# Hybrid attention, LRU and convolution trunk: the positions of the block compression as a block of their own

## The chip, the core and the metric

One core of one Trainium2 chip runs the whole program. The metric is device microseconds of one execution, the median over several runs. Engines are named as the profile names them: PE is TensorE (PEld its weight loads), DVE is VectorE, ACT is ScalarE, POOL is GpSimd, SP is SyncE, whose queue issues almost all DMAs.

## The reference, cut to what matters

Two layers, 512 tokens, model width 1024. Each layer normalises, projects to 4376 columns, and feeds three groups of heads (sparse attention, an RG-LRU, a Conformer convolution) that end in one output projection. The sparse attention compresses keys and values of overlapping blocks of 32 tokens, 16 apart (31 blocks, 2 groups of heads), with a position table that is the same for every block:

```python
    n_cmp = (T - L_CMP) // S_CMP + 1                      # 31
    idx = cmp_start[:, None] + jnp.arange(L_CMP)[None, :]
    def compress(kv, pos, w1, w2):
        blk = (kv[:, :, idx] + pos).reshape(B, N_KV, n_cmp, L_CMP * HEAD_DIM)
        return jax.nn.silu(blk @ w1) @ w2                 # w1: 2048 x 256, w2: 256 x 64
    kc = compress(k_c, cmp_pos[0], cmp_w1[0], cmp_w2[0])
    vc = compress(v_c, cmp_pos[1], cmp_w1[1], cmp_w2[1])
```

Since `pos` is the same for all blocks, `(kv + pos) @ w1` equals `kv @ w1` plus one row `pos @ w1` that is added to every block.

## The kernel before, in words

Everything is float32. A product that has to be exact to float32 is made of three matmuls on rounded parts: a matrix is split into a high part (a rounding copy on ACT, helper `cast`, L156) and a low part (the difference, on DVE, helper `lower`, L159). For weights, `w_split` makes both in tiles of 128 x 1024 called whi and wlo, three buffers each; one raw load of 1 MB (two buffers) yields two such pairs. A unit of projection (`proj`, L208 to 216) is 24 matmuls of 512 columns, eight times whi, whi, wlo, into one accumulator.

PE's order and that of all engines is, outside the attention, set by a scheduler of the build: it lists the instructions of each engine once, in advance, and each engine then works its list strictly in order. The code of a layer is written in the order of L981 to L1004: the gated units, q, the inputs of the compression (`do_kv`), keys, `do_prep(0)`, the LRU's inputs and gates (`do_u_lru`), `do_prep(1)`, `do_main(0)` with the four units of z_nsa between its parts, the LRU scan, `do_main(1)` with the units of z_lru, then the 30 taps for each of four channel tiles of the depthwise convolution (`conv_taps`, L422 on DVE, 120 a layer), which the scheduler spreads into whatever places DVE's list has.

The compression, for keys (c = 0) and values (c = 1):

- `do_prep(c)` turns the 32 x 64 position table by a transpose on PE (L639) and copies it into posT (L641, 128 x 16), and fetches the tokens into ee (called ce in the trace; rows are a token's parity and channel, columns the token pairs). For each half hf of the 16 token pairs of a block it adds posT to 31 overlapping windows of ee, once for each group of heads (L650, two instructions on DVE; neighbouring outputs are read 8 floats apart), and splits the sum cM into M (tile cMs; cast on ACT, lower at L655 on DVE): 62 high columns, 62 low columns for each of 8 token pairs j.
- `do_main(c)` multiplies: for each half, each j and each of whi and wlo, one matmul with M's 124 columns as weights and 256 columns of w1 moving (L675, 16 a half), all into one accumulator ph of 124 rows. It is copied (hs, L678), and a product with the 0/1 matrix `fold` (L681) adds the high row and the low row of a block and turns the result. What follows (L684 to L703) is the hidden layer's swish and the second product.

Around this on DVE: `u_lru` filters the LRU's inputs (L545), `gate` makes its gates (L578, L583), `do_scan` its products and scans (L589, L590), `z_nsa` closes the z_nsa units (L600). On ACT: L540, L542 evacuate the LRU's inputs, L574 to L582 its gates, L612 a square root, L599 the tanh of z_nsa.

Of the kernel before, what the change touches and what calls it, by code (L numbers as in the profile page):

```python
# [8 lines left out]
F32 = mybir.dt.float32  # L9
F32R = mybir.dt.float32r  # L10
# [3 lines left out]
OP = mybir.AluOpType  # L14
# [37 lines left out]
def tile_hybrid_trunk(ctx, tc, x_in, positions, norm_g, w_in, b_gate, cmp_pos, cmp_w1, cmp_w2, lru_conv_w,  # L52
# [4 lines left out]
    V, S, G, PE, SP = nc.vector, nc.scalar, nc.gpsimd, nc.tensor, nc.sync  # L57

    const = ctx.enter_context(tc.tile_pool(name="const", bufs=1))
# [8 lines left out]
    def big(name, dt=F32, tag="t"):  # L68
        return main.tile([128, 512], dt, name=name, tag=tag, bufs=TAGS[tag])

    def pair(name, dt=F32):
        return main.tile([128, 2, 512], dt, name=name, tag="p", bufs=TAGS["p"])
# [19 lines left out]
    for t in (ident, identb):  # L92
        G.affine_select(t, zeros[:, :128], pattern=[[1, 128]], compare_op=OP.not_equal, fill=1.0, base=0,
                        channel_multiplier=-1)
    G.memset(mask[:, :384], 0.0)
    G.affine_select(maskb, zeros[:, :128], pattern=[[-1, 128]], compare_op=OP.is_ge, fill=BIG, base=0,
                    channel_multiplier=1)
    G.affine_select(cmask, zeros[:, :128].rearrange("p (i n) -> p i n", i=4), pattern=[[128, 4], [-16, 32]],
                    compare_op=OP.is_ge, fill=BIG, base=-31, channel_multiplier=1)
    G.affine_select(seen, ones, pattern=[[0, 1]], compare_op=OP.is_ge, fill=0.0, base=-31, channel_multiplier=1)  # L100

    fold = const.tile([124, 2, 32], F32, name="fold")
    G.memset(fold, 0.0)
    for g in range(2):
        for half in range(2):
            G.affine_select(fold[:, g, :31], fold[:, g, :31], pattern=[[-1, 31]], compare_op=OP.not_equal, fill=1.0,
                            base=-31 * g - 62 * half, channel_multiplier=1)
    vcz = const.tile([128, 2, 2, 64], F32R, name="vcz")
    G.memset(vcz.bitcast(F32), 0.0)

# [44 lines left out]
    def cast(out, in_):  # L155
        S.copy(out, in_)  # L156

    def lower(out, in_, hi, eng=None):
        (eng or V).tensor_tensor(out, in_, hi.bitcast(F32), op=OP.subtract)  # L159
# [208 lines left out]
    def layer(l, X, o):  # L368
# [88 lines left out]

        def out_rows(X, t, n, W, M):
            p = acc()
            mh, ml = M  # L460
            m = 0
# [8 lines left out]

        def out_proj(X, kt0, M):

# [159 lines left out]
        CMP = {}  # L632

        def do_prep(c):

            pos = work.tile([16, 128], F32, name="pos", tag="oe", bufs=1)
            SP.dma_start(out=pos, in_=cmp_pos[l, c].rearrange("(j s) d -> j (s d)", s=2))
            pt = psum.tile([128, 16], F32, name="pt", tag="tr", bufs=2)
            PE.transpose(pt, pos, ident[:16, :16])  # L639
            posT = work.tile([128, 16], F32, name="posT", tag="posT", bufs=1)  # L640
            V.tensor_copy(posT, pt)  # L641
            ee = big("ce").rearrange("p (g m) -> p g m", g=2)
            for g in range(2):
                for s in range(2):
                    SP.dma_start(out=ee[s * 64:s * 64 + 64, g],
                                 in_=KV[c][g * 64:g * 64 + 64, s * 256:s * 256 + 256])
            for hf in range(2):
                m32 = big("cM")[:, :496].rearrange("p (j g n) -> p j g n", j=8, g=2)
                for g in range(2):
                    V.tensor_tensor(m32[:, :, g, :], ee[:, g, hf * 8:hf * 8 + 248].rearrange("p (n j) -> p j n", j=8),  # L650
                                    posT[:, hf * 8:hf * 8 + 8].unsqueeze(2).to_broadcast([128, 8, 31]), op=OP.add)
                m32 = m32.rearrange("p j g n -> p j (g n)")
                M = pair("cMs", F32R).rearrange("p a b -> p (a b)")[:, :992].rearrange("p (j n) -> p j n", j=8)
                cast(M[:, :, 0:62], m32)
                V.tensor_tensor(M[:, :, 62:124], m32, M[:, :, 0:62].bitcast(F32), op=OP.subtract)  # L655
                CMP[c, hf] = M

        def do_main(c, between):

            w2 = big("w2")[:, :256].rearrange("p (a o d) -> p a o d", a=2, o=2)  # L660
            for o in range(2 - c):
                SP.dma_start(out=w2[:, :, o, :], in_=cmp_w2[l, c].rearrange("(a p) d -> p a d", p=128))
            ph = psum.tile([128, 256], F32, name="pt", tag="tr", bufs=2)
            for hf in range(2):
                for _ in range(2):
                    next(between)
                r = raw_tile().rearrange("p (k c) -> p k c", c=256)
                SP.dma_start(out=r, in_=cmp_w1[l, c, hf * 1024:(hf + 1) * 1024, :].rearrange("(j p) c -> p j c", p=128))
                M = CMP[c, hf]
                for a in range(2):  # L670
                    hi, lo = w_split(r[:, 4 * a:4 * a + 4, :])
                    for k in range(4):
                        j = 4 * a + k
                        for w in (hi, lo):
                            PE.matmul(ph[:124], M[:, j], w[:, k], start=hf == 0 and j == 0 and w is hi,  # L675
                                      stop=hf == 1 and j == 7 and w is lo)
            hs = big("hs")[:124, :256]
            S.copy(hs, ph[:124])  # L678
            ph = psum.tile([128, 2, 64], F32, name="pt", tag="tr", bufs=2)
            for a in range(2):  # L680
                PE.matmul(ph[:, a], hs[:, a * 128:a * 128 + 128], fold.rearrange("p g n -> p (g n)"), start=True,  # L681
                          stop=True)
            hid = work.tile([128, 2, 64], F32, name="hid", tag="m")
            S.activation(hid, ph, AF.Tanh, scale=0.5)  # L684
            V.scalar_tensor_tensor(hid, hid, 1.0, ph, op0=OP.add, op1=OP.mult)
            if c == 0:
                pk = psum.tile([128, 2, 32], F32, name="pt", tag="tr", bufs=2)
                for a in range(2):
                    PE.matmul(pk.rearrange("p g n -> p (g n)"), w2[:, a].rearrange("p o d -> p (o d)"), hid[:, a, :],
                              start=a == 0, stop=a == 1)  # L690
                S.activation(KCH, pk, AF.Copy, scale=0.5)
                V.scalar_tensor_tensor(KCL, pk, 0.5, KCH.bitcast(F32), op0=OP.mult, op1=OP.subtract)
            else:
                pk = psum.tile([64, 64], F32, name="pt", tag="tr", bufs=2)
                for a in range(2):
                    PE.matmul(pk, hid[:, a, :], w2[:, a, 0, :], start=a == 0, stop=a == 1)

                for g in range(2):
                    b = slice(g * 32, g * 32 + 32)
                    S.activation(vcz[b, g, 0], pk[b], AF.Copy, scale=0.5)  # L700
                    V.scalar_tensor_tensor(vcz[b, g, 1], pk[b], 0.5, vcz[b, g, 0].bitcast(F32), op0=OP.mult,
                                           op1=OP.subtract)
                    S.copy(vcz[64 + g * 32:96 + g * 32, g], vcz[b, g].bitcast(F32))  # L703
# [284 lines left out]
        do_k()  # L988
        do_qs(1)
        do_prep(0)  # L990
        do_ks()
        do_u_lru()
# [51 lines left out]
```

## Time and profile before

| | |
|---|---|
| median of 3 runs | 774.03 us (773.87 to 775.85) |
| the profiled execution | 773.8 us, of which the span is 772.1 us |
| granted TensorE clock, mean | 0.998 of full |
| PE busy | 736.6 us, 95% of the span |
| DVE busy | 677.0 us, 88% |
| ACT busy | 460.3 us, 60% |
| POOL busy | 110.8 us, 14% |

The span starts with the first instruction and ends with the last; 1.7 us lie around it. A row of the timeline gives the start of a run of like instructions, how long they took together, the engine, line and operation, what was written from what, and in brackets the idle time of the engine just before with what ended it. Consecutive instructions of an engine overlap a little, so what one costs its queue is the distance from its start to the next start. All times of the text are of the first layer unless said; the second layer shows the same stretch 375 us later.

### The profile page before, as it was taken

What the parts mean: (1) busy time and instruction counts of PE and PEld (TensorE: products, weight loads), DVE (VectorE), ACT (ScalarE), POOL (GpSimd) and SP (SyncE); (2) the same over time, 40 slices, a digit from 0 to 9 for tenths busy, and PEclk for the clock granted to TensorE, in tenths of its full rate; (3) what the DMA queues carried; (4) which work ended last, traced back from release to release, by engine and by line L of the source; (5) the groups of instructions that cost most, each with busy time, mean ns of one, the idle gap of its engine ahead of it and who ended that gap; (6) DMA issues with size and microseconds to landing.
All of it is one profiled execution on the core that took longest, in us unless ns stands there. A gap on an engine that the chain in (4) does not pass through costs nothing.

```text
span 772.1 us, 10892 instructions
## 1 busy us (share of the span) xinstructions
PE 736.6 (95%) x3736; PEld 600.8 (78%) x3736; DVE 677.0 (88%) x1355; ACT 460.3 (60%) x891; POOL 110.8 (14%) x180
## 2 busy tenths in 40 slices
PE   7999999999999999999999999999999999999895
PEld 5788887677887787887798888776788787788774
DVE  5979999999997788988874999999999877899776
ACT  5443667684445567777652248669634375787663
POOL 2000000000001233444210000000000103344440
PEclk9999999999999999999999999999999999999999
DMA  6433285647441300103431334671855131010002
GB/s 216 137 110 106 58 212 133 178 137 248 127 154 61 113 2 2 54 2 87 168 111 56 109 104 116 191 199 34 265 182 164 54 106 59 1 56 1 2 27 110
DMA packets 68277, 82.01 MB, mean 106 GB/s; under 512 B 6633, under 2 KB 56873, under 8 KB 68222
## 3 DMA queue, kind: packets, MB, share of 16 engines
q1 hardware_dynamic: 68220, 81.31, 34.3%
q8 instruction: 30, 0.49, 0.3%
q14 instruction: 25, 0.20, 0.1%
q10 hardware_dynamic: 2, 0.00, 0.0%
HBM read 67.67 MB, written 4.19 MB: 93 GB/s over the span
## 4 chain that ended last, share of the span: by engine, by line
PE 70%; DVE 16%; ACT 8%; issue 4%; POOL 1%; DMA 1%; POOLq 0%; ACTq 0%; DVEq 0%
PE acc L214 44%; PE acc L464 9%; PE po L865 3%; PE pt L850 3%; ACT P L839 3%; PE acc L308 2%; DVE wlo L159 2%; PE ps L826 1%; PE ps L825 1%; DVE cv L422 1%; PE acc L763 1%; ACT whi L156 1%; DVE P L837 1%; PE pt L675 1%; DVE m L877 1%
## 5 line engine op out<-in xcount | busy, mean ns | idle before, releaser
L214 PE MATMUL acc<-H,whi 128*128 128x512 f32 x1024 | 325.6, 398 | 0.0
L214 PEld LDWEIGHTS acc<-H,whi 128*128 128x128 f32 x1024 | 191.4, 188 | 47.2 <-issue 1.9
L214 PE MATMUL acc<-H,wlo 128*128 128x512 f32 x512 | 203.6, 399 | 2.1 <-DVE wlo L159 2.1
L156 ACT CAST whi<-raw 128x1024 fp32r<-128x1024 f32 x102 | 106.7, 1050 | 161.4 <-PE acc L214 130.6
L422 DVE SCALAR_TENSOR_TENSOR cv<-sg,dww,cv 128x493 f32<-128x493 f32 (+18 forms) x240 | 165.4, 732 | 0.9
L159 DVE TENSOR_TENSOR wlo<-raw,whi 128x1024 fp32r<-128x1024 f32 x102 | 124.6, 1224 | 22.5 <-ACT whi L156 21.8
L214 PEld LDWEIGHTS acc<-H,wlo 128*128 128x128 f32 x512 | 96.3, 188 | 27.1 <-DVE wlo L159 3.5
L843 POOL TENSOR_SCALAR P<-P,hm,gt 128x384 f32<-128x384 f32 (+3 forms) x128 | 87.1, 687 | 131.4 <-DVE hm L841 114.7
L839 ACT ACTIVATE P<-P,hm 128x384 f32<-128x384 f32 (+2 forms) x96 | 59.0, 615 | 10.1 <-DVE hm L837 9.2
L221 POOL TENSOR_TENSOR mv<-mv,power 128x1 f32<-128x1 f32 x8 | 4.2, 546 | 419.2 <-DVE mv L725 419.2
L852 ACT CAST pt<-pt 128x512 fp32r<-128x512 f32 (+1 forms) x88 | 47.8, 546 | 23.5 <-PE pt L850 22.5
L853 DVE TENSOR_TENSOR pt<-pt 128x512 fp32r<-128x512 f32 (+1 forms) x88 | 55.7, 635 | 4.4 <-ACT pt L852 4.2
L837 DVE CUSTOM_DVE_ANT_0 P<-ps,mask 128x384 f32<-128x384 f32 (+2 forms) x96 | 51.9, 548 | 5.0 <-PE ps L826 4.4
L850 PE MATMUL pt<-ident,P 128*128 128x128 f32 x320 | 50.4, 274 | 5.0 <-DVE cs L787 3.9
L850 PEld LDWEIGHTS pt<-ident,P 128*128 128x128 f32 x320 | 38.6, 140 | 14.4 <-POOL P L843 5.7
L865 PEld LDWEIGHTS po<-pt,vv 128*128 128x128 f32 x304 | 43.8, 189 | 5.9 <-DVE pt L853 1.6
L865 PE MATMUL po<-pt,vv 128*128 128x256 f32 (+1 forms) x304 | 47.1, 289 | 0.7 <-DVE pt L853 0.7
L826 PE MATMUL ps<-KL,QS 128*128 128x384 f32 (+3 forms) x128 | 39.3, 322 | 0.0
L825 PE MATMUL ps<-KH,QS 128*128 128x384 f32 (+3 forms) x128 | 39.2, 321 | 0.0
L468 DVE TENSOR_TENSOR x<-x,acc 128x512 f32<-128x512 f32 x48 | 32.6, 680 | 0.6 <-PE acc L464 0.5
L464 PE MATMUL acc<-whi,mn 128*128 128x512 f32 x96 | 31.4, 406 | 0.3 <-DVE mn L881 0.3
L430 ACT COPY rs<-ru 32x512 f32<-32x512 f32 x48 | 29.7, 618 | 0.8
(242 smaller groups left out, 1213.1 us busy)
## 6 DMA issues: line engine op xcount, KB each, us to landing
raw<-in_w_in_dram SPq DMA_DIRECT2D x30, 1024.0 KB
raw<-in_w_out_dram SPq DMA_DIRECT2D x12, 1024.0 KB
raw<-in_cmp_w_dram SPq DMA_DIRECT2D x8, 1024.0 KB
x<-in_x_dram SPq DMA_DIRECT2D x8, 512.0 KB
raw<-in_w_in_dram SPq DMA_DIRECT2D x4, 512.0 KB
QS<-rs SPq DMA_DIRECT2D x8, 256.0 KB
QS<-ru SPq DMA_DIRECT2D x8, 256.0 KB
KH<-rs SPq DMA_DIRECT2D x8, 256.0 KB
```

What stands on the lines that cost most here:

```text
L156: S.copy(out, in_)
L159: (eng or V).tensor_tensor(out, in_, hi.bitcast(F32), op=OP.subtract)
L214: PE.matmul(p, w[k], h[k], start=n == 0, stop=n == 23)
L422: V.scalar_tensor_tensor(a[:, s:], u[:, :T - s], dww[:, ct, j:j + 1], a[:, s:], op0=OP.mult, op1=OP.add)
L464: PE.matmul(p, h[:, k], w, start=m == 0, stop=m == 11)
L837: V.tensor_tensor_reduce(p, sc[:, r, :], mask[:, 512 - L:], 1.0, BIG, OP.add, OP.min, hm[:, 0, r:r + 1])
L839: S.activation(p, p if i else sc[:, r, :], AF.Exp, scale=-1.0, bias=hm[:, 0, r:r + 1], accum_out=hm[:, 1, r:r + 1])
L843: G.tensor_scalar(P[:, r * L:(r + 1) * L], P[:, r * L:(r + 1) * L], hm[:, 2, r:r + 1], GA[i][:, h0 + r, 1 + b:2 + b], op0=OP.mult, op1=OP. ...
L850: PE.transpose(pt[:, kb, :], P[:, kb * 128:(kb + 1) * 128], ident)
L852: S.copy(dst[0], src)
L853: V.tensor_tensor(dst[1], src, dst[0].bitcast(F32), op=OP.subtract)
L865: PE.matmul(po, v, PT[w][:, kb].rearrange("p r q -> p (r q)"), start=False, stop=last and kb == i and w == 1)
```

## The change

The position table enters as a 32nd block of each group. M now has 128 columns for each j, ordered high/low, group, block: columns 0 to 30 of a group are the windows of ee, cast and lowered straight from ee for both groups in one instruction each, and column 31 is posT, cast and lowered in two small instructions of its own. The sum cM is gone. The matmuls of `do_main` then make, beside the 31 rows of blocks, a row of the positions, and `fold`, now 128 rows high, has ones that add row 31 of the first group (high and low) to all 62 blocks. Lines behind `fold` are two higher in the changed file, up to `do_prep`.

```diff
-    fold = const.tile([124, 2, 32], F32, name="fold")
+    fold = const.tile([128, 2, 32], F32, name="fold")
     G.memset(fold, 0.0)
-    for g in range(2):
-        for half in range(2):
+    for half in range(2):
+        for g in range(2):
             G.affine_select(fold[:, g, :31], fold[:, g, :31], pattern=[[-1, 31]], compare_op=OP.not_equal, fill=1.0,
-                            base=-31 * g - 62 * half, channel_multiplier=1)
+                            base=-64 * half - 32 * g, channel_multiplier=1)
+        G.affine_select(fold[:, :, :31], fold[:, :, :31], pattern=[[0, 2], [0, 31]], compare_op=OP.not_equal, fill=1.0,
+                        base=-64 * half - 31, channel_multiplier=1)
...
             for hf in range(2):
-                m32 = big("cM")[:, :496].rearrange("p (j g n) -> p j g n", j=8, g=2)
-                for g in range(2):
-                    V.tensor_tensor(m32[:, :, g, :], ee[:, g, hf * 8:hf * 8 + 248].rearrange("p (n j) -> p j n", j=8),
-                                    posT[:, hf * 8:hf * 8 + 8].unsqueeze(2).to_broadcast([128, 8, 31]), op=OP.add)
-                m32 = m32.rearrange("p j g n -> p j (g n)")
-                M = pair("cMs", F32R).rearrange("p a b -> p (a b)")[:, :992].rearrange("p (j n) -> p j n", j=8)
-                cast(M[:, :, 0:62], m32)
-                V.tensor_tensor(M[:, :, 62:124], m32, M[:, :, 0:62].bitcast(F32), op=OP.subtract)
-                CMP[c, hf] = M
+                M = pair("cMs", F32R).rearrange("p a b -> p (a b)").rearrange("p (j w g n) -> p j w g n", j=8, w=2, g=2)
+                for n, src in ((slice(0, 31), ee[:, :, hf * 8:hf * 8 + 248].rearrange("p g (n j) -> p j g n", j=8)),
+                               (slice(31, 32), posT[:, hf * 8:hf * 8 + 8].unsqueeze(2).unsqueeze(3)
+                                .to_broadcast([128, 8, 2, 1]))):
+                    cast(M[:, :, 0, :, n], src)
+                    lower(M[:, :, 1, :, n], src, M[:, :, 0, :, n])
+                CMP[c, hf] = M.rearrange("p j w g n -> p j (w g n)")
...
-                            PE.matmul(ph[:124], M[:, j], w[:, k], start=hf == 0 and j == 0 and w is hi,
+                            PE.matmul(ph, M[:, j], w[:, k], start=hf == 0 and j == 0 and w is hi,
                                       stop=hf == 1 and j == 7 and w is lo)
-            hs = big("hs")[:124, :256]
-            S.copy(hs, ph[:124])
+            hs = big("hs")[:, :256]
+            S.copy(hs, ph)
```

The scheduler also lists the instructions of this stretch in another order, on every engine. Three places show it. Names are those of the code with a number for each buffer; cv are the accumulators of the convolution, xc and rg the LRU's, zn the z_nsa results. In the changed file the lines L159, L422, L583, L589, L590 and L600 are L161, L424, L585, L591, L592 and L602.

DVE, from the first LRU scan of the layer on, before. wlo_1403 is the low part of the second half of the weights of the first compression product, wlo_1417 and wlo_1449 those of the third and the fourth z_nsa unit:

```order
L590 SCALAR_TENSOR_TENSOR xc0_1123<-xc0_1123,rg_1204 128x512
L590 SCALAR_TENSOR_TENSOR xc1_1159<-xc1_1159,rg_1204 128x512
L422 SCALAR_TENSOR_TENSOR cv2_695<-sg2_630,dww_392,cv2_695 128x501
L159 TENSOR_TENSOR wlo_1403<-raw_1388,whi_1402 128x1024
L583 SCALAR_TENSOR_TENSOR rr_1265<-sq_1288,rr_1265 128x512
L159 TENSOR_TENSOR wlo_1417<-raw_1414,whi_1416 128x1024
L650 TENSOR_TENSOR cM_1307<-ce_1302,posT_1300 128x8x31
L650 TENSOR_TENSOR cM_1313<-ce_1302,posT_1300 128x8x31
L159 TENSOR_TENSOR wlo_1449<-raw_1414,whi_1448 128x1024
```

The same place in the changed kernel, up to the third z_nsa unit (wlo_1405 and wlo_1419 are what wlo_1403 and wlo_1417 were):

```order
L592 SCALAR_TENSOR_TENSOR xc0_1127<-xc0_1127,rg_1208 128x512
L161 TENSOR_TENSOR cMs_1311<-posT_1304,cMs_1311 128x8x2
L592 SCALAR_TENSOR_TENSOR xc1_1163<-xc1_1163,rg_1208 128x512
L424 SCALAR_TENSOR_TENSOR cv2_701<-sg2_636,dww_398,cv2_701 128x503
L585 SCALAR_TENSOR_TENSOR rr_1269<-sq_1292,rr_1269 128x512
L424 SCALAR_TENSOR_TENSOR cv2_701<-sg2_636,dww_398,cv2_701 128x504
L161 TENSOR_TENSOR wlo_1405<-raw_1390,whi_1404 128x1024
L161 TENSOR_TENSOR wlo_1419<-raw_1416,whi_1418 128x1024
```

A small lowering of the positions, one more tap and the gate's product now stand ahead of the low weights, and the taps are two further on (503 where 501 was).

DVE, directly behind that, in the changed kernel; wlo_1451 is what wlo_1449 was:

```order
L424 SCALAR_TENSOR_TENSOR cv2_701<-sg2_636,dww_398,cv2_701 128x505
L591 SCALAR_TENSOR_TENSOR rg_1270<-rg_1270,rr_1269 128x512
L161 TENSOR_TENSOR cMs_1311<-ce_1306,cMs_1311 128x8x2x31
L161 TENSOR_TENSOR cMs_1316<-ce_1306,cMs_1316 128x8x2x31
L161 TENSOR_TENSOR cMs_1316<-posT_1304,cMs_1316 128x8x2
L592 SCALAR_TENSOR_TENSOR xc2_1201<-xc2_1201,rg_1270 128x512
L591 SCALAR_TENSOR_TENSOR rg_1270<-rg_1270,rr_1269 128x512
L602 SCALAR_TENSOR_TENSOR zn_1356<-zn_1356,acc_1331 128x512
L602 SCALAR_TENSOR_TENSOR zn_1356<-zn_1356,acc_1363 128x512
L161 TENSOR_TENSOR wlo_1451<-raw_1416,whi_1450 128x1024
```

Two instructions stood between the low weights of the third and of the fourth unit; now nine do.

PE at the second half of the first compression product in the changed kernel (before, all 16 matmuls of L675 stood together, and the first two matmuls of both the third and the fourth unit behind them):

```order
L675 MATMUL pt_1324<-whi_1404,cMs_1070 128x256
L216 MATMUL acc_1422<-H00_126,whi_1418 128x512
L216 MATMUL acc_1422<-H10_128,whi_1418 128x512
L675 MATMUL pt_1324<-wlo_1405,cMs_1070 128x256
```

and where the fourth unit begins, 22 matmuls of the third unit later:

```order
L216 MATMUL acc_1454<-H00_126,whi_1450 128x512
L216 MATMUL acc_1454<-H10_128,whi_1450 128x512
L675 MATMUL pt_1324<-whi_1483,cMs_1075 128x256
L216 MATMUL acc_1454<-H00_126,wlo_1451 128x512
```

Two matmuls of the third unit moved ahead of the seven that need wlo_1405; the fourth unit's third matmul in this list needs wlo_1451.

## Rows read from the trace of the kernel before

**Rows 1.** The page, part 1: busy time, share of the span, instructions.
```profile
PE 736.6 (95%) x3736; PEld 600.8 (78%) x3736; DVE 677.0 (88%) x1355; ACT 460.3 (60%) x891; POOL 110.8 (14%) x180
```
**Rows 2.** Busy time by stretches: length, PE, PEld, DVE, ACT, POOL, clock, DMA, GB/s.
```profile
155.00:165.00 10.00, 8.54 (x43) 6.97 (x42) 10.00 (x14) 9.92 (x13) 0.00 (x0) 1.00 0.05 13
165.00:175.00 10.00, 10.00 (x47) 8.13 (x46) 10.00 (x16) 8.10 (x10) 0.00 (x0) 1.00 0.91 297
```
**Rows 3.** Waits of PE, whole span: us in total, times, longest.
```profile
PE pt L675 <- DVE wlo L159: 2.9, 2, 1.5
...
PE acc L214 <- DVE wlo L159: 2.1, 2, 1.1
```
**Rows 4.** Timeline of PE: start, us, instruction, count, idle before.
```profile
164.59 0.38 PE L675 MATMUL pt<-wlo,cMs 128*124 128x256 f32 x1 [1.46 <-DVE wlo L159]
...
166.44 0.40 PE L214 MATMUL acc<-H,wlo 128*128 128x512 f32 x1
...
176.70 0.28 PE L675 MATMUL pt<-whi,cMs 128*124 128x256 f32 x1
...
178.49 0.28 PE L675 MATMUL pt<-wlo,cMs 128*124 128x256 f32 x1
...
180.79 0.50 PE L214 MATMUL acc<-H,wlo 128*128 128x512 f32 x1 [1.04 <-DVE wlo L159]
```
**Rows 5.** Timeline of DVE, from the fourth LRU channel tile on.
```profile
147.79 0.75 DVE L545 SCALAR_TENSOR_TENSOR xc<-lu,prm,xc 128x509 f32<-128x509 f32 x1
...
159.83 0.68 DVE L589 SCALAR_TENSOR_TENSOR rg<-rg,rr 128x512 f32<-128x512 f32 x1
160.43 2.33 DVE L590 TENSOR_TENSOR_SCAN xc<-xc,rg 128x512 f32<-128x512 f32 x2
162.68 0.72 DVE L422 SCALAR_TENSOR_TENSOR cv<-sg,dww,cv 128x501 f32<-128x501 f32 x1
163.31 1.22 DVE L159 TENSOR_TENSOR wlo<-raw,whi 128x1024 fp32r<-128x1024 f32 x1
164.45 0.68 DVE L583 SCALAR_TENSOR_TENSOR rr<-sq,rr 128x512 f32<-128x512 f32 x1
165.05 1.22 DVE L159 TENSOR_TENSOR wlo<-raw,whi 128x1024 fp32r<-128x1024 f32 x1
...
173.06 1.87 DVE L600 SCALAR_TENSOR_TENSOR zn<-zn,acc 128x512 f32<-128x512 f32 x3
```
**Rows 6.** Timeline of ACT.
```profile
146.97 0.79 ACT L542 ACTIVATE xc<-acc,prm 128x512 f32<-128x512 f32 x1
...
160.74 1.04 ACT L156 CAST whi<-raw 128x1024 fp32r<-128x1024 f32 x1
```
**Rows 7.** Durations by line or tile: ns min/median/max, first and last start, forms.
```profile
L650 DVE TENSOR_TENSOR cM<-ce,posT x16: 631/647/683, 123.8 to 544.1; 128x248 f32<-128x248 f32 x16
L655 DVE TENSOR_TENSOR cMs<-cM,cMs x8: 660/680/701, 128.3 to 545.8; 128x496 fp32r<-128x496 f32 x8
...
L156 ACT CAST cMs<-cM x8: 602/612/615, 127.5 to 544.8; 128x496 fp32r<-128x496 f32 x8
...
L641 DVE COPY posT<-pt x4: 164/167/172, 121.3 to 517.5; 128x16 f32<-128x16 f32 x4
...
L799 DVE TENSOR_TENSOR cp<-cp,sm x8: 415/421/426, 265.7 to 735.0; 128x256 f32<-128x256 f32 x8
```
**Rows 8.** Timeline of PE in the attention: matmuls with 128-column weights.
```profile
335.51 1.10 PE L865 MATMUL po<-pt,vv 128*128 128x256 f32 x8
```
**Rows 9.** Timeline of POOL and of SP's queue.
```profile
3.14 0.70 POOL L106 TENSOR_SCALAR_AFFINE_SELECT fold<-fold 124x31 f32<-124x31 f32 x4
5.76 0.55 POOL L221 TENSOR_TENSOR ss<-ss,power 128x1 f32<-128x1 f32 x1 [1.93 <-DVE ss L353]
...
168.55 0.37 SPq L171 DMA_DIRECT2D raw<-in_w_in_dram x1
```
**Rows 10.** The chain of work that ended last, in order of time.
```profile
181.29 0.39 PE pt L681 x4
```

## The prediction

> **What bounds the kernel.** I read the page first, then the busy time by stretches, the waits and the timelines of PE and DVE. PE is busy 95% of the span [rows 1], so time is gained or lost where PE waits, or where it has more to do. The place of the change shows such waits. Between 155 and 165 us DVE is busy 10.00 of 10 us and ACT 9.92, while PE has 8.54 [rows 2]: PE is short of operands there, and the two engines that make them are full. PE's waits name the operand: it waits for wlo, the low part of weights, at the compression product, twice in the span [rows 3]. In the first layer that is 1.46 us until 164.59, and again 1.04 us until 180.79 at a z unit [rows 4]. The second layer does the same, so the stretch costs 2.5 us a layer, 5.0 in all. DVE's list says why: the wlo that PE needs starts at 163.31, right behind two scans and a tap, with no idle time before it [rows 5], although the high part it is subtracted from was cast at 160.74 to 161.78 [rows 6]. In this stretch PE's time is the sum of DVE's list.
>
> **The parts without effect on the path.** PE's weights have 128 columns in place of 124. The 16 matmuls of a half start 0.119 us apart (176.70 to 178.49) [rows 4]; eight with 128 columns and as many moving columns take 1.10 us, 0.117 apart after the last one's 0.28 [rows 4, 8]. That adds nothing. The taller copy hs and the taller fold product move the same number of columns. POOL gets two more selects of `fold`, at 0.18 each by the four that take 0.70; POOL then idles 1.93 us before the first norm needs it [rows 9]. Without that cover the start would be 0.4 later. The number of DMAs is unchanged. The load of the next z weights, issued at 168.55 [rows 9], needs the buffer that the fourth unit's wlo releases, and on SP's queue it also falls behind one tile of x; with the times below it goes out at about 174.9, takes 3.5 us by 1 MB at 297 GB/s [rows 2], and ACT can use it only from 180.0. If it came later than that, it would replace the last wait below.
>
> **What the new instructions cost.** Of the old sum, an instruction of 248 elements took 0.65 us; one of 256 with the same kind of broadcast operand but neighbouring reads took 0.42 [rows 7]. So the broadcast costs nothing and the reads 8 floats apart cost 0.23 for 248. On its queue an instruction costs 0.08 less than its duration (1.22 from 163.31, next start 164.45) [rows 5]. The new lowering has 496 such reads: 0.60 (L655's 0.68 less 0.08) plus twice 0.23, 1.06. Its bounds are 0.60, if the reads cost nothing there, and 1.14, twice an L650. I take 1.06, since the reads are the same ones. [...] The small instructions for the positions I price by the copy of posT, 0.16 less overlap, about 0.10 [rows 7], 0.17 at most. For each half DVE loses two L650 (0.57 each) and an L655 (0.60), 1.74, and gains 1.16: 0.6 us saved, eight times. ACT's cast, 0.61 before [rows 7], may take up to 1.1 with those reads; it has 1.9 of 10 us free between 165 and 175 [rows 2], so two of them and two small ones (1.3 more) fit there.
>
> **The order decides.** All of that saving would be PE's if the lists kept their order. They don't.
> - *Up to the fourth LRU tile.* From the copy of posT (121.3 us) [rows 7] to the first filter step of that tile (147.79) [rows 5] DVE loses four L650 and two L655, 3.48, and gains two lowerings and two small ones, 2.32; but two taps of 0.63 (162.68 to 163.31) [rows 5] are drawn in ahead, 1.26, and ACT's small cast of the positions stands ahead of copies that DVE waits for, 0.17. Together +0.27: it starts at about 148.06. Earlier than 147.76 it can't, since ACT's L542 writes its operand until then [rows 6].
> - *To the second half's low weights.* Before, 15.52 us from there to 163.31 [rows 5]. Now a tap (0.63), the gate's product (0.60) and a small lowering (0.10) are ahead: start 148.06 + 15.52 + 1.33 = 164.91, end 166.13, PE goes on at 166.19 in place of 164.59. ACT casts the high part behind two gate steps of at most 0.79 [rows 6] and the small cast, from 162.5 at the latest; that is in time. Seven matmuls take PE 0.92 (1.85 to 166.44 [rows 4] less four of 0.233, the spacing of the 44 up to 176.70); the next wlo, right behind, lets it go on at 167.33.
> - *To the fourth unit's low weights.* 22 matmuls of 0.233, two more and one of 0.12: PE wants wlo_1451 at 173.05. On DVE a wlo (1.14), a tap, two LRU products (1.20), two lowerings (2.12), a small one, a scan (1.13) and two L600 (1.20) stand ahead: 166.05 + 7.52 = 173.57, end 174.79, PE at 174.85. **That is a new wait of 1.80 us**, where PE had none. Behind it 22 matmuls and 15 of the product end at 181.77, against 178.61 before (178.49 + 0.12): 3.16 late.
> - *To the z unit's low weights.* DVE: three wlo (3.42), two L600 (1.20), a scan, five taps (3.15): start 173.57 + 8.90 = 182.47, PE goes on at 183.75, after a wait of 0.9 that answers to the old 1.04. By then PE has also done the fold product, 0.39 [rows 10], which came behind this wait before. Delay 183.75 - 0.39 - 180.79 = 2.57.
>
> Behind this the list is as before, and DVE, lighter, has slack. Two layers: **5.1 us slower**. The profiled execution (773.8: span 772.1 and 1.7 around it) would be 778.9; the median of the runs is 0.2 above it, so 779.2. With the lowering at 0.60 the first step is held at 147.79 by ACT, the later ones gain another 0.92, and the delay is 1.38 a layer: 776.8. With 1.14 and small ones of 0.17 it is 3.2 a layer: 780.4.
>
> **The rivals.**
> - *Faster, 769.0.* DVE and ACT are the engines PE waits for, and DVE is relieved; if that reached PE, both old waits would go, 5.0 us. [...] The point at which it decides is the low weights of the second half: they would have to be there when PE arrives, at 163.13 (164.59 less 1.46) [rows 4], 1.4 us earlier than before. Against it: the fourth LRU tile pins DVE at 147.76, and only things that were added stand between.
> - *No change, 774 to 776.3.* The lowering costs 0.60 and DVE makes up another 0.4 a layer, because the drawn-in taps are missing later and the last wait shrinks; or the attention, where PE has short waits of its own, takes part of the delay. For it: the 0.9 at the last step is short. Against it: PE has no more idle time than 5% [rows 1].
>
> **How the numbers follow.** A measurement here tells about 0.3%, 2.3 us, from no change: faster is below 771.7, slower above 776.35. My forecast has 0.78, no change 0.13, faster 0.09. The range reaches from 775.0, inside the case of no change, to 782.0: the upper bound of 780.4 and one more wait of 0.8 a layer, since what ACT and the loads do in the new order is known by bounds only.
>
> **What would show it.** Waits of PE on wlo in the projection units rise from 1.04 us a layer to about 3, the longest near 1.8, some 10 us behind the first compression product begins; the lowering from ce reads about 1.15 us; DVE's busy time falls by some 5 us, ACT's rises by 2 to 5. The step is wrong if the first wait ends before 165.5 or the fourth unit's wlo starts before 172; then DVE isn't the sum I take it for. If the wlo come late as computed but the span doesn't grow, the delay is given back later.

## The result and the profile after

| | before | after |
|---|---|---|
| median of the runs | 774.07 us (773.87 to 775.85, 4 runs) | 781.17 us (779.78 to 781.37, 4 runs) |
| the profiled execution, and its span | 773.8, 772.1 | 779.78, 777.6 |
| granted TensorE clock, mean | 0.998 | 0.996 |

The ratio is 1.0084, 95% interval 1.0072 to 1.0097: slower, as forecast (779.2; range 775.0 to 782.0), and by more than the forecast said. Busy time on the page of the changed kernel, which answers to [rows 1]:

```profile
PE 740.3 (95%) x3736; PEld 602.1 (77%) x3736; DVE 672.3 (86%) x1347; ACT 465.3 (60%) x899; POOL 110.8 (14%) x182
```

DVE has 4.7 us less to do and ACT 5.0 more; the kernel has become slower with less work on the engine that PE waits for. PE's busy time rose by 3.7 with the same 3736 matmuls, which is explained below. PE's waits in the whole span (us, times, longest), against [rows 3]:

```profile
PE pt L675 <- DVE wlo L161: 2.2, 2, 1.1
...
PE acc L216 <- ACT whi L158: 1.7, 4, 0.6
...
PE acc L216 <- DVE wlo L161: 1.3, 2, 1.1
...
PE pt L675 <- ACT whi L158: 0.5, 2, 0.3
```

The waits on wlo add up to 3.5 us, where they were 5.0: by this view alone the kernel should be faster. What happened is on PE's timeline of the second layer (all rows of the stretch with idle time ahead of them, and three that the text uses: the third unit's first low weights, the lone matmul at 551.28, and the z unit's first low weights):

```profile
541.41 0.38 PE L675 MATMUL pt<-whi,cMs 128*128 128x256 f32 x1 [0.23 <-ACT whi L158]
542.36 0.74 PE L216 MATMUL acc<-H,whi 128*128 128x512 f32 x2 [0.56 <-ACT whi L158]
544.17 0.39 PE L675 MATMUL pt<-wlo,cMs 128*128 128x256 f32 x1 [1.07 <-DVE wlo L161]
...
545.30 0.50 PE L216 MATMUL acc<-H,wlo 128*128 128x512 f32 x1
...
551.28 0.38 PE L675 MATMUL pt<-whi,cMs 128*128 128x256 f32 x1
552.81 0.51 PE L216 MATMUL acc<-H,wlo 128*128 128x512 f32 x1 [1.14 <-DVE wlo L161]
...
561.41 0.50 PE L216 MATMUL acc<-H,whi 128*128 128x512 f32 x1 [0.29 <-ACT whi L158]
561.77 0.50 PE L216 MATMUL acc<-H,wlo 128*128 128x512 f32 x1
```

PE now stops five times a layer where it stopped twice [rows 4], at operands of both engines. The same stretch by windows, from the first matmul of the first compression product to the z unit's second pair of high weights: first the kernel before, then the changed one (length, PE busy, its matmuls; then PEld, DVE, ACT, POOL, clock, the share of the DMA engines, GB/s).

```profile
536.99:556.57 19.58, 17.03 (x89) 13.86 (x88) 19.58 (x26) 14.02 (x18) 0.00 (x0) 1.00 0.66 215
```
```profile
540.08:562.11 22.03, 18.58 (x90) 14.19 (x89) 22.03 (x28) 16.05 (x21) 0.00 (x0) 1.00 0.60 200
```

The stretch holds the same work and became 2.45 us longer: 0.90 of it is idle time of PE and 1.55 is "busy". A matmul of 256 columns inside a run starts 0.12 after the one ahead of it, and the row of one that stands alone shows 0.38 (541.41, 551.28); each stop so hides part of the delay in busy time. The delay can't be read from the idle time of PE, only from what DVE's list does. DVE is busy in all 22.03 us. Its rows at the operands (first layer, then the second):

```profile
148.92 0.75 DVE L547 SCALAR_TENSOR_TENSOR xc<-lu,prm,xc 128x509 f32<-128x509 f32 x1
...
165.67 2.36 DVE L161 TENSOR_TENSOR wlo<-raw,whi 128x1024 fp32r<-128x1024 f32 x2
167.94 0.74 DVE L424 SCALAR_TENSOR_TENSOR cv<-sg,dww,cv 128x505 f32<-128x505 f32 x1
...
169.20 2.07 DVE L161 TENSOR_TENSOR cMs<-ce,cMs 128x496 fp32r<-128x496 f32 x2
...
174.18 1.24 DVE L161 TENSOR_TENSOR wlo<-raw,whi 128x1024 fp32r<-128x1024 f32 x1
...
542.90 2.35 DVE L161 TENSOR_TENSOR wlo<-raw,whi 128x1024 fp32r<-128x1024 f32 x2
...
551.54 2.35 DVE L161 TENSOR_TENSOR wlo<-raw,whi 128x1024 fp32r<-128x1024 f32 x2
...
560.50 2.35 DVE L161 TENSOR_TENSOR wlo<-raw,whi 128x1024 fp32r<-128x1024 f32 x2
```

To price the stretch in every kernel I use two landmarks on ACT, ahead of it and behind it: the evacuation of the fourth LRU channel tile (L542 before, L544 after) and the last evacuation of the z_conv units of the layer (L628, L630). Before, then after:

```profile
231.82 0.59 ACT L628 ACTIVATE zc<-acc 128x512 f32<-128x512 f32 x1
...
522.09 0.79 ACT L542 ACTIVATE xc<-acc,prm 128x512 f32<-128x512 f32 x1
...
606.85 0.58 ACT L628 ACTIVATE zc<-acc 128x512 f32<-128x512 f32 x1
```
```profile
147.82 0.79 ACT L544 ACTIVATE xc<-acc,prm 128x512 f32<-128x512 f32 x1
...
235.13 0.59 ACT L630 ACTIVATE zc<-acc 128x512 f32<-128x512 f32 x1
...
525.14 0.79 ACT L544 ACTIVATE xc<-acc,prm 128x512 f32<-128x512 f32 x1
...
612.46 0.59 ACT L630 ACTIVATE zc<-acc 128x512 f32<-128x512 f32 x1
```

With 146.97 for the first layer before [rows 6] the changed kernel is late by 0.85, 3.31, 3.05 and 5.61: **the stretch costs 2.46 and 2.56 us**, 5.02 of the 5.98 us between the two profiled executions. 0.85 lies ahead of it, 0.48 outside the span (2.18 against 1.7), and 0.37 is given back elsewhere.

### The profile page after: what moved, and what is told of

It is laid out like the page before. It is cut to its first block, busy times and chain, and to the rows that moved or that the text cites. A ratio compares the mean times of both kernels' runs of the same rounds, so it can differ in the third digit from the quotient of the medians.

```text
span 777.6 us, 10898 instructions
## 1 busy us (share of the span) xinstructions
PE 740.3 (95%) x3736; PEld 602.1 (77%) x3736; DVE 672.3 (86%) x1347; ACT 465.3 (60%) x899; POOL 110.8 (14%) x182
## 4 chain that ended last, share of the span: by engine, by line
PE 62%; DVE 23%; ACT 8%; issue 4%; DMA 1%; POOL 1%; POOLq 0%; DVEq 0%; ACTq 0%
PE acc L216 36%; PE acc L466 9%; DVE cv L424 4%; PE po L865 3%; PE pt L850 3%; DVE wlo L161 3%; PE acc L310 2%; ACT P L839 2%; DVE xc L547 2%; ACT whi L158 2%; PE ps L826 2%; PE ps L825 1%; PE pt L675 1%; PE acc L763 1%; DVE P L837 1%
## 5 line engine op out<-in xcount | busy, mean ns | idle before, releaser
L424 DVE SCALAR_TENSOR_TENSOR cv<-sg,dww,cv 128x489 f32<-128x489 f32 (+20 forms) x240 | 165.9, 730 | 1.1
L161 DVE TENSOR_TENSOR wlo<-raw,whi 128x1024 fp32r<-128x1024 f32 x102 | 124.2, 1222 | 31.2 <-ACT whi L158 30.6
L310 PE MATMUL acc<-wv,H 128*128 128x280 f32 x192 | 28.9, 306 | 1.8 <-DVE wv L161 1.4
```

Source lines behind the costliest of these rows:

```text
L424: V.scalar_tensor_tensor(a[:, s:], u[:, :T - s], dww[:, ct, j:j + 1], a[:, s:], op0=OP.mult, op1=OP.add)
```

## The experiments

The theory (A in the expectations): each engine works its list in order, so the time is lost where the new order puts work ahead of the low weights on DVE; the far reads of the two lowerings there cost part of it. The rivals: the far reads alone; the order of the taps alone; the 128 columns, the taller copy and the taller `fold`. The table has all runs, against the kernel before on the same chip (medians 774.07 us for the change, and 775.35, 775.08 and 775.7 for the three sets e1 to e4, e5 to e8, e9 to e11); times of different sets are therefore compared by their ratios. The cost of a layer is what the lateness grows between the landmarks, in us, in the profiled execution; in e5, e6 and e9 it holds falls of PE's clock, told below. The first layer of the change holds one as well (0.57 from 167 to 171 us), and costs about what the second does.

| run | what | us | ratio, 95% | layer 1, 2 |
|---|---|---|---|---|
| the change | | 781.17 | 1.0084 (1.0072 to 1.0097) | 2.46, 2.56 |
| e1_near | change, reads side by side | 778.92 | 1.0042 (1.0026 to 1.0058) | 1.77, 1.65 |
| e2_old_order | change, DVE in the order of before | 775.56 | 1.0003 (0.9991 to 1.0015) | -0.20, -0.08 |
| e3_near_old_order | both | 771.84 | 0.9956 (0.9941 to 0.9971) | -1.42, -1.39 |
| e4_before_near | before, reads side by side | 774.10 | 0.9985 (0.9973 to 0.9998) | -0.98, -0.90 |
| e5_taps_late | change, eight taps behind the z unit's wlo | 795.83 | 1.0274 (1.0259 to 1.0290) | 9.43, 10.92 |
| e6_wlo_early | change, fourth unit's wlo early | 795.37 | 1.0266 (1.0251 to 1.0281) | 9.93, 10.35 |
| e7_before_128 | before, 128 columns and rows | 775.30 | 1.0007 (0.9999 to 1.0016) | -0.07, -0.02 |
| e8_best | e3, second half's wlo between the scans | 774.72 | 0.9997 (0.9987 to 1.0007) | -0.43, -0.57 |
| e9_wlo_with_cast | change, fourth unit's whi and wlo early | 780.97 | 1.0082 (1.0067 to 1.0097) | 3.98, 3.95 |
| e10_taps_as_before | change, without the taps drawn in | 779.36 | 1.0060 (1.0045 to 1.0074) | 1.69, 1.69 |
| e11_best2 | e3, two wlo early, the cast too | 771.61 | 0.9959 (0.9946 to 0.9972) | -1.69, -1.55 |

**The reads (e1_near, e4_before_near).** The inputs of the compression are stored so that the windows lie side by side; nothing else moves in any list. In the changed kernel:

```diff
-                dv = d.rearrange("p (s m) -> p m s", s=2)
+                dv = d.rearrange("p (s j n) -> p n j s", s=2, j=8)
...
-                for n, src in ((slice(0, 31), ee[:, :, hf * 8:hf * 8 + 248].rearrange("p g (n j) -> p j g n", j=8)),
+                for n, src in ((slice(0, 31), ee.rearrange("p g (j n) -> p j g n", j=8)[:, :, :, hf:hf + 31]),
```

and the same storage with L650's reads in the kernel before.

> The changed kernel with one layout altered: the K and V rows lie as (s, j, n), so that the casts and the lowerings from ce read neighbouring floats; all five engines keep the changed kernel's order. Theory A (the order of DVE's list makes the waits, the strided reads only lengthen them): the lowering falls from 1.13 to about 0.68 us, the cast from 1.19 to about 0.61; two lowerings stand ahead of the fourth unit's low weights, so of the 3.16 us at the end of the second product about 0.9 go, 1.2 a layer by the end of the list: 778.8 us, still slower than before. Rival B (the price of the strided reads is the whole loss): 774 or less.

> The kernel before with the layout (s, j, n) alone, so that its eight sums of positions read neighbouring floats; the order of every engine is that of before. Theory A: each sum falls from 0.65 to about 0.42 us; the four of them that stand behind the first wait take 0.9 off the second wait of 1.04 a layer, those ahead of it nothing, since ACT pins the list there: 772.2 us. Rival B (the price of the reads passes through in full, 8 times 0.23 a layer): 770.3.

The groups by form, first of the changed kernel, then of e1 (busy, mean ns, idle before), and L650 in e4, which took 647 [rows 7]:

```profile
L158 ACT CAST cMs<-ce 128x496 fp32r<-128x496 f32 x8 | 9.0, 1173 | 0.0
L161 DVE TENSOR_TENSOR cMs<-ce,cMs 128x496 fp32r<-128x496 f32 x8 | 8.8, 1124 | 0.0
```
```profile
L161 DVE TENSOR_TENSOR cMs<-ce,cMs 128x496 fp32r<-128x496 f32 x8 | 5.2, 669 | 0.0
L158 ACT CAST cMs<-ce 128x496 fp32r<-128x496 f32 x8 | 4.4, 602 | 0.0
```
```profile
L650 DVE TENSOR_TENSOR cM<-ce,posT 128x248 f32<-128x248 f32 x16 | 6.1, 419 | 0.0
```

The same instruction on the same elements costs 0.46 us more on DVE and 0.57 more on ACT when its reads are 8 floats apart. What in the reads makes them dearer was not shown.

PE goes on accordingly earlier at the fourth unit's low weights in e1's second layer:

```profile
543.00 0.39 PE L675 MATMUL pt<-wlo,cMs 128*128 128x256 f32 x1 [1.09 <-DVE wlo L161]
...
550.71 0.50 PE L216 MATMUL acc<-H,wlo 128*128 128x512 f32 x1 [0.61 <-DVE wlo L161]
```

On the path the reads are worth 0.8 us a layer in the change (2.46 and 2.56 against 1.77 and 1.65) and 0.9 in the kernel before. So they are a part of the loss and not the whole. e4 came out at 774.10, 1.25 under the kernel before on its chip, where 1.9 was expected, though its stretches gained what they should. Its profiled execution is late by 1.97 at the first landmark already, and shows a clock that was granted less in other places (the windows' columns are as above):

```profile
0.00:30.00 30.00, 23.58 (x114) 19.23 (x115) 19.40 (x49) 16.40 (x27) 5.38 (x24) 0.94 0.61 191
640.00:670.00 30.00, 27.89 (x158) 23.76 (x157) 23.14 (x68) 19.35 (x52) 9.78 (x14) 0.94 0.00 1
```

Such falls come and go from execution to execution of one kernel, and in most sets the longer executions are those with the lower mean clock (the kernel before beside e1 to e4: spans of 771.8 to 773.1 at 0.998, 775.5 at 0.993). The layer's cost is free of those that lie outside the stretch.

**The order (e2_old_order, e3_near_old_order).** DVE's instructions from the gated units to z_conv are tied to the order of before, by an edge without a wait from each to the next; the small lowerings stand next to the large ones. e3 has the reads side by side as well.

```diff
+        made = [i for i in nc.cur_bb.bb.instructions[first:] if i.engine == mybir.EngineType.DVE]
+        for a, b in zip(ORDER, ORDER[1:]):
+            tc.add_manual_dep(made[b], made[a].name, mybir.DependencyInfo(
+                mybir.DependencyClass.NoSync, mybir.DependencyReason.DATA), reason="order")
```

> The changed kernel with its strided reads, DVE held to the order of the kernel before: each new lowering stands where the old subtraction stood, no tap and no gate product is drawn in ahead. Theory A: the first wait on wlo stays near 1.46 us, since ACT pins DVE's first filter step of the fourth LRU tile; behind it DVE has 1.16 us a layer less to do, so the second wait of 1.04 goes: 2.0 under the kernel before, about 772 us, and 8 or 9 under the changed kernel. Rival B (the price of the reads): the order alone wins nothing, 779 to 781 us. Rival C (the taller product and fold, or something at the start of the program, costs the time): 779 to 781 us too, but with the waits on wlo small.

> Both edits together: reads of neighbouring floats and DVE in the order of the kernel before. Theory A: DVE has 2.1 us a layer less than before behind the first wait; the second wait is gone already with 1.16, so little more is won than by the order alone: 771 to 772 us. Rival B: about 774.

With DVE's order alone undone, the loss of 2.5 us a layer is gone: the order is its cause. The far reads cost in either order; the kernel before pays for them too (e4). But e2 doesn't gain what DVE saves, against its expectation. PE's and DVE's timelines of e2 in the first layer (its low weights are L170, its units L225, its compression product L684) show what holds it:

```profile
164.08 0.39 PE L684 MATMUL pt<-whi,cMs 128*128 128x256 f32 x1 [0.19 <-ACT whi L167]
165.02 0.74 PE L225 MATMUL acc<-H,whi 128*128 128x512 f32 x2 [0.56 <-ACT whi L167]
165.59 0.28 PE L684 MATMUL pt<-wlo,cMs 128*128 128x256 f32 x1
...
167.21 0.50 PE L225 MATMUL acc<-H,wlo 128*128 128x512 f32 x1 [0.16 <-DVE wlo L170]
...
181.17 0.50 PE L225 MATMUL acc<-H,wlo 128*128 128x512 f32 x1 [1.10 <-DVE wlo L170]
```
```profile
169.41 1.15 DVE L170 TENSOR_TENSOR cMs<-ce,cMs 128x496 fp32r<-128x496 f32 x1 [0.39 <-ACT cMs L167]
```

The stop at the second half's low weights stays, though no row shows a wait for them: PE takes them up 17.72 us after the landmark (147.87 to 165.59), before 17.62 (146.97 to 164.59). PE's list, which the edit doesn't tie, has two matmuls of the third unit ahead of them, and the old wait of 1.46 is now two short waits on whi and matmuls that stand alone. The wait at the z unit stays as well (1.10 for 1.04): DVE waits 0.39 for ACT, whose casts of M have grown, and from the second half's wlo to the z unit's it saves 0.52 (164.20 to 179.90 for 163.31 to 179.53) of the 1.16 expected. In e3 casts and lowerings are short, the same way takes DVE 14.42 (164.52 to 178.94) for 16.22, and the wait at the z unit is gone. The stop at the second half stays there too (17.72 after the landmark); PE waits 0.19 and 0.56 on whi and 0.17 on the third unit's wlo, and nothing more in the stretch. e3 is faster than both kernels, and shows what the change, with its reads side by side, could have been. From e2 to e3 the reads are worth 1.2 and 1.3 us a layer, more than in e1; DVE's wait for ACT's casts goes with them.

**The rows (e7_before_128).** The kernel before, its DVE and ACT held to its own order, with 32 columns a block of windows and a column of zeros:

```diff
+                G.memset(M[:, :, :, :, 31:32].bitcast(F32), 0.0)
...
-                            PE.matmul(ph[:124], M[:, j], w[:, k], start=hf == 0 and j == 0 and w is hi,
+                            PE.matmul(ph, M[:, j], w[:, k], start=hf == 0 and j == 0 and w is hi,
```

> The kernel before in the order of before, with the 128-row layout alone: 32 columns per block group, the 32nd set to zero on GpSimd, a fold of 128 rows and a 128-row copy; the positions are still added to every block. Theory A: as the kernel before, within 1 us. Rival C (the taller product, fold or copy costs time): 1 us or more slower. The part of an execution outside the span shows where the 0.4 us come from that all kernels with the new work have there (2.1 in place of 1.7): 2.1 if from the fold or the layout, 1.7 if not.

Its layers cost -0.07 and -0.02: 128 columns in place of 124, the taller copy and the taller fold product cost nothing. That rival is out.

**Which part of the order (e5_taps_late, e6_wlo_early, e9_wlo_with_cast, e10_taps_as_before).** All four hold DVE and ACT to the order of the change and move some instructions in it; the edits are shown by the lists in short. e5 moves eight taps:

```diff
 xc<-xc,rg
-tap 503
 rr<-sq,rr
-tap 504
 wlo (second half), wlo (third unit)
-tap 505
...
 zn<-zn,acc
 wlo, wlo (z unit)
+taps 503, 504, 505, 506, 487, 507, 488, 508
 hid<-hid,pt
```

> The changed kernel with its strided reads; DVE and ACT held to its own order, but for eight taps of the convolution that stand between the scans and the low weights of the first z unit: they now follow those. Theory A (the drawn-in taps are what makes the order dear): the low weights of the second half start two taps sooner (1.3 us), those of the fourth unit three (1.9), those of the z unit eight (5.1), so that only a first wait and about 0.9 at the fourth unit stay: about level with the kernel before, 775 to 776 us, where the changed kernel takes 781. Rival B (the strided reads): at most 0.6 a layer is won, 780. Rival D (the place of a single lowering, not the sum ahead of it): 779 to 781.

e5 missed by far. DVE's timeline (its taps are L438) has idle time now, and then a block that nothing may pass; ACT's has what comes of it:

```profile
182.43 0.69 DVE L616 SCALAR_TENSOR_TENSOR zn<-zn,acc 128x512 f32<-128x512 f32 x1 [2.10 <-ACT zn L615]
...
186.09 5.67 DVE L438 SCALAR_TENSOR_TENSOR cv<-sg,dww,cv 128x503 f32<-128x503 f32 x8
```
```profile
192.88 0.22 ACT L705 ACTIVATE kc<-pt 128x64 fp32r<-128x64 f32 x1 [6.61 <-PE pt L703]
```

The taps are filler: the scheduler puts them where DVE would wait for an operand. Taken out, they leave idle time there, and put in one block they stand 5.67 us ahead of the small steps between the compression's products, for which ACT waits with its next casts and PE with those. Beside that, the granted clock was 0.50 from 204 to 208 us, inside the stretch (on the mean of the execution 0.985, before 0.998), so a part of e5's cost is that of a slower PE.

> The changed kernel, DVE and ACT held to its own order, but for one lowering: the low weights of the fourth unit stand right behind the next two wlo, ahead of the new lowerings, a scan and two L602, 6.2 us sooner. Theory A (PE's time is the sum of DVE's list up to the z unit): the wait at the fourth unit goes and the second product ends 1.5 us sooner, but the list up to the z unit's low weights is as long as it was; PE waits there instead, no gain: 780.5 to 781.5 us. Rival D (the wait at the fourth unit is the loss): 1.1 to 1.5 a layer won, 778 to 779.

e6 moves the fourth unit's wlo directly behind the third's, on DVE alone. I had overlooked that ACT casts its high part far later; DVE waits there for 4.93 us, with all that is behind:

```profile
172.62 1.23 DVE L175 TENSOR_TENSOR wlo<-raw,whi 128x1024 fp32r<-128x1024 f32 x1 [4.93 <-ACT whi L172]
```

Here, too, the clock fell inside the stretch (0.50 from 188 to 192 us, on the mean of the execution 0.985), so that wait isn't the whole cost.

e9 moves the cast on ACT as well:

```diff
 ACT: sq<-xc
-whi, whi
+whi, whi, whi
...
 DVE: tap 504
-wlo, wlo
+wlo, wlo, wlo
```

> The changed kernel, DVE and ACT held to its own order but for one pair of instructions: the cast of the fourth unit's high weights follows the third unit's cast on ACT (before the second square root's table load), and the lowering of its low weights follows the third unit's on DVE, so that this time it finds its cast done. Theory A (PE's time is the sum of DVE's list up to the z unit): the wait at the fourth unit goes, but the list up to the z unit's low weights is as long as before, so at most 0.3 a layer is won: 780.5 to 781.5 us. Rival D (the place of this lowering is the loss): 1.1 to 1.5 a layer, 778 to 779.

The wait at the fourth unit is gone, and its time is not won: PE waits at the z unit, on wlo, as its timeline shows.

```profile
184.66 0.50 PE L230 MATMUL acc<-H,wlo 128*128 128x512 f32 x1 [1.76 <-DVE wlo L175]
```

DVE's list up to the z unit's low weights is as long as before the move: PE takes them up 36.72 us after the landmark (147.94 to 184.66), in the change 36.62 (147.82 to 184.44). That e9's layer cost, 3.98, is above the change's 2.46 has another reason, behind this point: in the first layer PE's granted clock fell to 0.57 there, and in the second two matmuls of 512 columns from 566.13 took 1.20 us, where two from 568.66 took 0.63. The window in the first layer, e9 and then the change:

```profile
186.00:190.00 4.00, 4.00 (x14) 3.32 (x13) 2.78 (x5) 0.22 (x1) 0.00 (x0) 0.57 0.79 258
```
```profile
186.00:190.00 4.00, 4.00 (x21) 3.34 (x20) 3.58 (x6) 0.23 (x1) 0.00 (x0) 1.00 0.90 276
```

By an estimate from these rows, 4 us at 0.57 do the work of 2.3 at full clock; the 1.7 lost is about the 1.5 between the two costs. The medians are alike all the same: e9's profiled execution, 782.67, is the slowest of its five, the change's, 779.78, the fastest of its four.

e10 leaves out the taps that the change draws in between the scans and the fourth unit's wlo (503, 504, 505), and goes on behind that wlo in the order of before.

> The changed kernel, DVE in its own order up to the scan behind the fourth unit's low weights, without the taps that were drawn in ahead of that point; from there on DVE goes in the order of the kernel before, so that these taps stand where they stood before. ACT is held to the changed order up to the copy hs. Theory A: the low weights of the second half start 1.3 us sooner, those of the fourth unit 0.6 sooner (their cast on ACT ends then), those of the z unit about 1.3 sooner: 1.0 a layer won, 778.5 to 779.5 us. If the drawn-in taps alone were the loss, as the fifth run's expectation had it: 775 to 776. Rival B (the strided reads): no gain, 781.

It wins 0.8 us a layer of the 2.5. What PE waits for then is ACT:

```profile
172.89 0.74 PE L229 MATMUL acc<-H,whi 128*128 128x512 f32 x2 [0.94 <-ACT whi L171]
```

So the taps alone aren't the cause either. That the rest lies in where the lowerings stand and in ACT's longer list beside them follows only from what is left over: no run moves those alone.

**A faster version (e8_best, e11_best2).** Both start from e3. e8 moves the second half's wlo ahead of the second scan and its cast ahead of the last gate's step; e11 moves two and has the cast earlier (DVE's list in short):

```diff
 DVE: xc<-xc,rg (first scan)
+wlo (second half)
 xc<-xc,rg (second scan)
+wlo (third unit)
 tap 501
-wlo (second half)
 rr<-sq,rr
-wlo (third unit)
```

> Reads of neighbouring floats and DVE in the order of before as in the third run, and one lowering more is moved: the low weights of the product's second half stand between the two scans, and ACT casts their high part ahead of the last gate's L580 steps. Theory A: of PE's three short waits there (0.19, 0.56 and 0.17 a layer) most go, so 1 to 1.8 us under the third run's 771.8: 770.0 to 770.8. Rival: PE's next operand is as late (the casts of the high parts on ACT stand close together), and the waits only move: 771.5 to 772.

> The third run's kernel (neighbouring reads, DVE in the order of before) with two lowerings moved ahead: those of the product's second half and of the third unit stand right behind the first and the second of the two scans, and ACT, held to the third run's order, casts the first one's high part right behind the exponential of the last gate. Theory A: each lowering finds its cast done and DVE idles for neither; of PE's 0.92 us of waits a layer in the third run 0.2 to 0.4 stay: 770.5 to 771 us. Rival: as in the eighth run a wait of DVE for a cast takes their place: 772 to 775.

e8 lost 1.0 and 0.8 us a layer against e3: DVE reaches the moved wlo before the cast is there (162.87, idle 0.80), and PE waits at the third unit:

```profile
164.15 0.39 PE L685 MATMUL pt<-wlo,cMs 128*128 128x256 f32 x1 [0.62 <-DVE wlo L171]
...
167.66 0.50 PE L226 MATMUL acc<-H,wlo 128*128 128x512 f32 x1 [1.42 <-DVE wlo L171]
```

e11 moves both, and PE's only wait up to the z unit is 0.23 us on whi. A layer costs 0.2 to 0.3 less than in e3, but the time is level with e3's (ratios 0.9959 and 0.9956); the 1 us expected didn't come. Both beat the kernel before by 0.4%.

## Why the prediction was right, and where it wasn't

- **The bound, right.** The forecast took PE's time in this stretch to be the sum of DVE's list, in the order that the change gives it. e2, which undoes DVE's order and nothing else, takes the 2.5 us a layer away; e9, which takes the wait at the fourth unit away but leaves the list as long, wins nothing up to the z unit. Neither sign of a wrong step came: the first wait ended at 166.94, and the fourth unit's wlo started at 174.18.
- **The list, right to 0.15.** All of it began 0.86 later than worked out (the start is told below): the fourth tile's first filter step at 148.92 for 148.06, the second half's wlo at 165.67 for 164.91 (0.10 off). From one low part to the next, with the start shift gone: fourth unit 8.64 (layer 2) and 8.51 (layer 1) for 8.66; PE from the second half's wlo to the fourth unit's 8.64 (544.17 to 552.81) for 8.66, and to the z unit's 17.60 (561.77) for 17.56. The delay was 2.46 and 2.56 a layer for 2.57.
- **The lowering, right.** 1.12 us for "about 1.15"; e1 shows that its reads are the reason. What they are worth on the path was over-estimated: with 0.60 in place of 1.06 the delay was to be 1.38 a layer, 1.2 less; e1 gives 0.7 to 0.9. The 0.92 of the two lowerings between the second half's and the fourth unit's wlo came (PE goes on 7.71 later in e1's second layer, 8.64 in the change's); the 0.27 at the first step hardly did: from the landmark to PE's going on at the second half's wlo it is 18.97 us in e1 (524.03 to 543.00) and 19.03 in the change (525.14 to 544.17).
- **"That is a new wait of 1.80 us": the delay right, the sign to look for wrong.** The row shows 1.14 in the second layer and 0.18 in the first. PE's stream of matmuls ends 0.46 after 550.53, at about 551.0, and it goes on at 552.81, 1.8 later; but a lone matmul of 0.38 stands in between, and its gap and its own duration take the rest. In the first layer the clock, 0.57 from 167 to 171 us, filled the time with slower matmuls (below). The "about 3" us of waits on wlo in the units that I wanted to see came out as 1.3 for both layers together.
- **"after a wait of 0.9 that answers to the old 1.04", wrong in its kind.** At the z unit PE waits 0.29 for ACT's whi, and not for wlo. It goes on at the forecast time nevertheless. The z unit's low weights start at 560.50 and take about 1.2, and PE takes them up at 561.77: DVE's list still sets the time, and the stops in front of it, longer than forecast, have used up the wait.
- **Left out: the waits on whi,** 0.23 to 0.28 and 0.56, ahead of the second half's wlo. The sum had the casts "in time". They cost nothing there, since wlo comes later still; e10, where PE waits 0.94 for a later cast, shows that ACT is next.
- **The columns, the copy, the fold: right,** by e7.
- **The rest of the difference.** The sum for the profiled execution was 778.9 and it took 779.78: 5.02 for 5.1 in the layers, and 0.85 at the start and 0.48 outside the span, both of which the sum had at nothing, less 0.37 elsewhere. Of the 0.85, 0.54 is there where DVE casts the tokens' positions for the rotary tables (L132, now L134), for whose load it waits: at 18.73 us before, 19.27 after, and between 19.16 and 20.11 in e1 to e4. In e4 the start of the program is that of the kernel before, so this is not the change's doing alone. POOL's cover for the longer `fold` held: it still idles 1.39 us before the first norm. The other runs of the change have spans of 778.9 to 779.3 at clocks of 0.993 to 0.994, 1.3 to 1.7 above the profiled one. So the median came out 2.0 above the forecast: 0.9 by the profiled execution, the rest goes with the other runs' lower clock, which the sum left out.

## What to carry to other kernels

Work taken off an engine that others wait for doesn't reach the end by itself (here DVE had 4.7 us less to do, and the execution took 5.98 longer): where a build lists the instructions in advance, the freed places are filled with other work, and the price of a change is the length of the new list up to each operand, so compare the lists operand by operand. Idle time of the waiting engine understates a delay when the engine is stopped more often, because lone matmuls show their whole duration as busy (here 0.38 us, where one inside a run starts 0.12 after the last; of 2.45 us lost 0.90 were idle). Before a step is moved earlier on one engine, find when its operand is made on the other; e6 and e8 lost by that (DVE idle for 4.93 and 0.80 us).

## What the runs showed of the hardware beside this

The granted clock in the first layer of the change, by windows of the profiled execution:

```profile
164.00:167.00 3.00, 1.16 (x4) 0.54 (x4) 3.00 (x5) 2.97 (x4) 0.00 (x0) 1.00 0.00 0
167.00:171.00 4.00, 4.00 (x14) 3.47 (x15) 4.00 (x5) 3.97 (x6) 0.00 (x0) 0.57 0.62 202
171.00:174.00 3.00, 3.00 (x14) 2.41 (x14) 3.00 (x6) 2.88 (x4) 0.00 (x0) 1.00 0.69 257
```

PE was busy for 1.16 of 3 us, then ran at 0.57 of full speed for four microseconds that are all busy, and then at full speed again. It cost nothing: 14 matmuls took those 4 us, and PE came to an operand that wasn't there yet; the second layer, at a clock of 1.00, lost the same 2.5. In e9 PE was busy for 1.13 us of the same three, and the clock stayed at 1.00 behind them, so these stops alone don't decide it. Where it did fall in e9, from 186 to 190 us, PE had been busy for 2.08 of the 4 us before, and behind it PE had no operand left to wait for: the fall cost about 1.5 us.

The time outside the span is 1.7 to 1.8 us in all runs of the kernel before, in e4 and in e7, 2.0 to 2.2 in the change, e1, e2, e3, e8 and e11, and 1.7 to 2.2 in e5, e6, e9 and e10. e7 shows that it isn't the taller `fold`; what it is was not tried.
